# Two thirds of a depthwise convolution's taps as ScalarE products that VectorE adds, and a fifth seven-product pair in four early groups

## The chip, the cores and the metric

One Trainium2 chip, one core of it. The metric is the device time of one launch in microseconds, taken as the median of three runs. TensorE (PE), its weight loads (PEld), VectorE (DVE), ScalarE (ACT), GpSimd (POOL) and the DMA queue of SyncE (SP) each run their own instruction list in order and meet through semaphores.

## The reference, cut to what matters

```python
xn = rms_norm(h, norm_in_g)                       # 256 x 4096, float32
q, k, v, z_a, a_c, g_c, z_c = split(xn @ w_in)    # each 256 x 2048
y_a = rms_norm(chunked_attention(q, k, v), attn_out_g) * silu(z_a)

u = a_c * sigmoid(g_c)                            # convolution module
u = pad(u, 30 rows in front)
u = depthwise_conv(u, w_dw) + b_dw                # 31 taps a channel, causal
u = silu(layer_norm(u)) @ w_pw + b_pw
y_c = rms_norm(u, conv_out_g) * silu(z_c)

h = h + concat(y_a, y_c) @ w_out
h = h + sigmoid(rms_norm(h) @ w_ple_gate + b) * (p @ w_ple)
out = rms_norm(h, final_g)
```

256 rows, a width of 4096, 16 heads of 128. The change is in the taps of the depthwise convolution and in how four of the products `xn @ w_in` are computed.

## The kernel before

**Products.** Every big product is float32 by halves. A weight tile `wt` (128 rows, two column blocks of 512) is rounded by ScalarE to `wh` (`nc.scalar.copy`, L204), VectorE takes the rest `wl = wt - wh` (L205), and PE makes three matmuls of 128x512 for each block: high by high, low by high, high by low (L385). `wh` and `wl` have three buffers each, `wt` five.

**Groups.** `mixed_product` makes two column blocks at a time for both halves of the 256 rows. Its 4096 rows of weights go in 16 *pairs* of two 128-row blocks. A plain pair takes 2 x 4 x 3 = 24 matmuls. A pair with a mark in the order (`0+`, `4*`) is done in Winograd's way by seven products in place of eight: 7 x 3 = 21 matmuls, for which sums of weight blocks, `ua` and `ub`, are made first and split into `uh` and `ul`. With `*` VectorE makes the sums `ua` (L467, L468); with `+` a second DMA with accumulation, issued by GpSimd, does (L420, L421). The sums `ub` (L474, L475) are VectorE's in both. The other operand of such a pair is a combination of the blocks of xn, kept in `xS`; the combinations for pairs 8 and 10 come later than the others, from `more_combinations`.

**Stages.** The first part of the kernel is ten groups: `glu_conv(0)`, `glu_conv(1)`, q and k of heads 0 to 3, v of heads 0 to 7, then attention on heads 0 to 3, `glu_conv(2)`, and so on to the ninth, `heads((o_q, 3), (o_v, 2), order=early_five)`, and the tenth, which has the order `norm`. `glu_conv(1)` and the `heads` groups have the order `early` (four marked pairs, all `+`), `glu_conv(2)` and `(3)` `early_six` (six), the ninth `early_five` (five). Pointwise product, gated output, `w_out` and `w_ple_gate` follow, which the change does not touch.

**The convolution.** Each `glu_conv(c)` ends with the gated input transposed into `uT` (128 channels x 4 blocks x 256 rows) and puts 4 x 31 calls of `conv_tap` into the queue `later`: one VectorE instruction per block and tap, `cv += uT * dw` with the tap's weight as a per-channel scalar (L724; the first tap, with the bias, is L720). `fill(n)` takes the next n calls; `mixed_product` calls it after every pair, with the counts of `early_fills` or `six_fills`.

**What sets the order.** The program order is a wish: a scheduler at build time places each engine's instructions by when it takes them to be ready, so taps may move ahead of where `fill` puts them. `queued_behind(made)` keeps what is made in it behind given instructions; `recent` holds the last `wh` cast and the last `wl`. On each engine the order is fixed once built.

**Memory.** `home` is the tag `hd` with five buffers of 128 x 4 x 256, for `uT`, `kT`, `v`, the bias of the attention and sums. `stage` has two buffers, for the `z` of a group. `act` has eight buffers, for `cv`, `qT` and the late combinations `comb_x`.

Of the kernel before, what the change touches and what calls it, by code (L numbers as in the profile page):

```python
# [10 lines left out]
F32 = mybir.dt.float32  # L11
F32R = mybir.dt.float32r
AF = mybir.ActivationFunctionType
ALU = mybir.AluOpType
AX = mybir.AxisListType

P = 128
# [8 lines left out]
def hybrid_block(  # L26
# [23 lines left out]
    nc = tc.nc  # L50
    _, T, D = x.shape
# [5 lines left out]
    TAPS = w_dw.shape[1]  # L57
    PAD = TAPS - 1
# [23 lines left out]
    spool = pool("spool", 2, first_scratch, 1)  # L82
# [11 lines left out]
    o_q, o_k, o_v, o_za = 0, AW, 2 * AW, 3 * AW  # L94
# [85 lines left out]
    later = deque()  # L180

    def fill(n):
        for _ in range(min(n, len(later))):
            later.popleft()()
# [27 lines left out]
    recent = []  # L212

    @contextmanager
    def queued_behind(made):

        with ExitStack() as queued:
            for ins in made:
                queued.enter_context(tc.issue_after(ins.ins))
            yield  # L220
# [111 lines left out]
    early_five = units("1 3 5 0+ 7 9 2+ 11 4* 13 6+ 15 8* 10 12 14")  # L332
    early_six = units("1 3 5 0+ 7 2* 9 4+ 11 6* 13 8+ 15 10* 12 14")

    early_fills = (5, 6, 1, 5, 6, 1, 5, 6, 1, 5, 6, 1, 2, 5, 5, 4)
    six_fills = (6, 6, 1, 5, 1, 5, 1, 5, 1, 5, 1, 5, 1, 6, 7, 7)
    norm = units("1 3 5 7 9 11 0+ 13 2* 15 4+ 8 6* 10 12 14")
    norm_fills = (7, 8, 8, 8, 6, 4, 2, 3, 2, 3, 2, 2, 0, 6, 5, 5)
# [167 lines left out]
    tt, stt = nc.vector.tensor_tensor, nc.vector.scalar_tensor_tensor  # L506
# [174 lines left out]
    taps = w_dw[0].rearrange("t (b j q) -> (t b) j q", j=DWC, q=P)  # L681
# [10 lines left out]
    dw = spool.tile([P, KCW, TAPS], F32, name="dw", bufs=1)  # L692
# [25 lines left out]
    def conv_tap(cv, uT, i, b, k):  # L718
# [4 lines left out]
        else:  # L723
# [2 lines left out]
                cv[:, i, PAD - k :], ALU.mult, ALU.add,  # L726
            )

    def more_combinations(pair):

        if pair in (7, 9):
            c = (pair + 1) // 2
            xS[2 * c] = act.tile([P, 2, 2, T], F32R, tag="act", name="comb_x"), 0
            later.extendleft(reversed(combinations(c)))

    def glu_conv(c):
        if c == 0:
            sg, gate = scaled_pair(
                w_in0, o_a, o_g - o_a, first, r_x, (1,), begin=first_pairs
            )  # L740
        else:
            sg, gate = scaled_pair(
                w_in0, o_a + c * NB, o_g - o_a,
                *((early, r_x, early_fills) if c == 1 else (early_six, r_x, six_fills)),
                ahead=more_combinations if c == 2 else None,
            )
        for h in range(NH):
            nc.scalar.activation(gate[:, h, :], gate[:, h, :], AF.Sigmoid)
            tt(sg[:, h, :], sg[:, h, :], gate[:, h, :], ALU.mult)
        uT = spool.tile([P, 4, T], F32, tag="hd", name="uT", bufs=5)  # L750
        for pair in range(2):
            pt = tmp_psum()
            for i in range(2):
                for h in range(NH):
                    b = 2 * pair + i
                    nc.tensor.transpose(
                        pt[:, i * T + h * P : i * T + (h + 1) * P],
                        sg[:, h, b * P : (b + 1) * P],
                        ident,
                    )  # L760
            nc.scalar.copy(
                uT[:, 2 * pair : 2 * pair + 2, :], pt.rearrange("q (i t) -> q i t", t=T)
            )
        cv = act.tile([P, 4, T], F32, tag="act", name="cv")
        for i in range(4):
            for k in reversed(range(TAPS)):
                later.append(partial(conv_tap, cv, uT, i, 4 * c + i, k))
        conv.append(cv)


# [174 lines left out]
    home = dict(tag="hd", bufs=5)  # L945
# [9 lines left out]
    def heads(*parts, order=None, fills=early_fills, **kw):  # L955

        cols = [o + g * NB for o, g in parts]
        tiles = scaled_pair(
            w_in0, cols[0], cols[1] - cols[0], order or early, r_x, fills,
            homes=[home if o == o_v else dict(tag="stage") for o, _ in parts], **kw  # L960
        )
        for (o, g), t in zip(parts, tiles):
            if o == o_v:
                vs[g] = t
            else:
                (queries_of if o == o_q else keys_of)(g, t)
# [6 lines left out]

    n_g = H // GH
    assert n_g == CW // NB == 4
    glu_conv(0)
    glu_conv(1)
    load_bias(0)
    heads((o_q, 0), (o_k, 0))
    heads((o_v, 0), (o_v, 1))  # L980
    attention(0)
    glu_conv(2)
    load_bias(1)
    heads((o_q, 1), (o_k, 1))
    attention(1)
    glu_conv(3)
    load_bias(2)
    heads((o_q, 2), (o_k, 2))
    heads((o_q, 3), (o_v, 2), order=early_five)
    attention(2)  # L990
    layer_norm_swish()
# [24 lines left out]
    spool = upool = pool("lpool", 2, side=1)  # L1016
# [109 lines left out]
    for c0 in range(0, D // NB, 2):  # L1126
        for j in range(2):
            hc = act.tile([P, NH, NB], F32, tag="act", name="hc")
            c = c0 + j
# [5 lines left out]
        def on_helpers(helper):  # L1135
# [10 lines left out]
            ahead=y_ahead if c0 == 0 else before_last(h_ahead) if c0 + 2 == D // NB else None,  # L1146
            fills=(2,),
# [114 lines left out]
    def weigh(h, j):  # L1262
        pin(tt(z[h][j], hs[c0 + j][:, h, :], fgs[j], ALU.mult))
# [41 lines left out]
    halves = [slice(i * NB // 2, (i + 1) * NB // 2) for i in range(2)]  # L1305
# [46 lines left out]
```

## Time and profile before

| | |
|---|---|
| median of three runs | 2029.14 us (2028.86 to 2029.4) |
| the profiled execution | 2028.23 us |
| its span, first to last instruction | 2026.5 us |
| the second to ninth group with two attentions, 97.2 to 793.7 us of the span | 696.5 us |
| DMA, mean of the span | 215 GB/s |
| granted TensorE clock, mean | 0.998 |

All durations below come from the profiled execution. A row of a group view gives the operation, how many there are, their busy time together, the mean of one in ns, and the engine's idle time before them with what ended it. A row of the time line gives start, length, engine, line and operation, the number of instructions merged, and in brackets idle time before. Two instructions of one engine can overlap at their ends, so a merged row can be shorter than its number times the mean.

### The profile page before, as it was taken

How to read it: one execution, taken by the hardware profiler on the slowest of the kernel's cores; microseconds unless marked ns; L12 is line 12 of the kernel's file. 1: busy time of each engine (PE TensorE's matmuls, PEld its weight loads, DVE VectorE, ACT ScalarE, POOL GpSimd, SP SyncE). 2: the span in 40 equal slices, each digit the busy share in tenths (PEclk: the TensorE clock that was granted, in tenths of full speed). 3: DMA queues.
4: the chain of work that ended last, by engine and by line, in shares of the span. 5: the costliest groups of instructions: out<-in, count | busy, mean ns of one | idle time of the engine just before them, and what ended most of it. 6: DMA issues, size and time to landing. Idle time of an engine off the chain costs nothing.

```text
span 2026.5 us, 26195 instructions
## 1 busy us (share of the span) xinstructions
PE 2010.8 (99%) x9073; PEld 1654.4 (82%) x9073; DVE 1903.4 (94%) x2708; ACT 1215.0 (60%) x1583; POOL 46.9 (2%) x50
## 2 busy tenths in 40 slices
PE   9999999999999999999999999999999999999997
PEld 7888888888888888788888888888888888888876
DVE  7999999889999997888899999999999999999998
ACT  7655545655655555776556556666665666655555
POOL 0000000000000000000000000000000000000000
PEclk9999999999999999999999999999999999999999
DMA  8787878678678867456666666676666656666765
GB/s 295 222 238 234 255 217 250 177 247 240 188 221 246 252 198 241 156 177 209 196 208 207 208 204 211 208 239 210 203 211 197 208 194 201 208 218 207 231 207 180
DMA packets 171168, 436.70 MB, mean 215 GB/s; under 512 B 13966, under 2 KB 17182, under 8 KB 171034
## 3 DMA queue, kind: packets, MB, share of 16 engines
q1 hardware_dynamic: 161952, 417.93, 63.9%
q0 software_dynamic: 8432, 16.25, 4.8%
q8 instruction: 71, 1.16, 0.2%
q10 hardware_dynamic: 650, 0.84, 0.1%
q14 instruction: 63, 0.52, 0.1%
HBM read 430.77 MB, written 4.19 MB: 215 GB/s over the span
## 4 chain that ended last, share of the span: by engine, by line
PE 95%; DVE 3%; issue 1%; ACT 1%; DMA 0%; POOLq 0%; POOL 0%; ACTq 0%; SPq 0%; DVEq 0%
PE acc L385 73%; PE acc_P L385 17%; PE tmp_ps L170 1%; DVE cv L724 1%; PE acc L229 1%; DVE wl L205 1%; PE tmp_ps L893 0%; PE tmp_ps L877 0%; PE tmp_ps L911 0%; PE tmp_ps L916 0%; PE acc L373 0%; ACT wh L204 0%; PE tmp_ps L892 0%; DVE ul L205 0%; DMA xin<-in_x_dram 0%
## 5 line engine op out<-in xcount | busy, mean ns | idle before, releaser
L385 PE MATMUL acc<-wh,big_t 128*128 128x512 f32 x4154 | 1283.3, 391 | 0.6 <-DVE y_c L1043 0.4
L204 ACT CAST wh<-wt 128x1024 fp32r<-128x1024 f32 (+1 forms) x737 | 710.1, 974 | 523.3 <-PE acc L385 364.3
L385 PEld LDWEIGHTS acc<-wh,big_t 128*128 128x128 f32 x4154 | 777.0, 188 | 160.8 <-DVE y_c L1043 0.9
L205 DVE TENSOR_TENSOR wl<-wt,wh 128x1024 fp32r<-128x1024 f32 (+1 forms) x737 | 817.4, 1122 | 39.9 <-ACT wh L204 33.6
L385 PE MATMUL acc<-wl,big_t 128*128 128x512 f32 x2077 | 801.9, 391 | 0.1
L385 PEld LDWEIGHTS acc<-wl,big_t 128*128 128x128 f32 x2077 | 389.5, 188 | 82.5 <-DVE wl L205 1.8
L204 ACT CAST uh<-ua 128x1024 fp32r<-128x1024 f32 x174 | 182.9, 1052 | 91.1 <-DVE ua L468 46.3
L205 DVE TENSOR_TENSOR ul<-ua,uh 128x1024 fp32r<-128x1024 f32 x174 | 212.0, 1219 | 9.6 <-ACT uh L204 8.1
L724 DVE SCALAR_TENSOR_TENSOR cv<-uT,dw,cv 128x250 f32<-128x250 f32 (+19 forms) x480 | 203.6, 464 | 1.1
L385 PE MATMUL acc_P<-uh,big_t 128*128 128x512 f32 x528 | 161.8, 392 | 0.0
L204 ACT CAST uh<-ub 128x1024 fp32r<-128x1024 f32 x92 | 96.8, 1052 | 95.5 <-DVE ub L475 79.2
L205 DVE TENSOR_TENSOR ul<-ub,uh 128x1024 fp32r<-128x1024 f32 x92 | 112.2, 1220 | 6.7 <-ACT uh L204 5.6
L385 PEld LDWEIGHTS acc_P<-uh,big_t 128*128 128x128 f32 x528 | 98.0, 188 | 23.2 <-ACT uh L204 3.7
L385 PE MATMUL acc_P<-ul,big_t 128*128 128x512 f32 x264 | 101.3, 392 | 0.0
L467 DVE TENSOR_TENSOR ua<-wt 128x512 f32<-128x512 f32 x102 | 69.9, 685 | 17.3 <-DMA wt<-in_w_in_dram 10.7
L385 PE MATMUL acc<-uh,big_t 128*128 128x512 f32 x266 | 82.5, 390 | 0.0
L385 PE MATMUL acc_P<-wh,big_t 128*128 128x512 f32 x266 | 82.1, 389 | 0.0
L468 DVE TENSOR_TENSOR ua<-wt 128x512 f32<-128x512 f32 x102 | 69.6, 683 | 4.3 <-DMA wt<-in_w_in_dram 3.6
L385 PE MATMUL acc_P<-uh,comb_t 128*128 128x512 f32 x228 | 70.1, 390 | 0.1
L475 DVE TENSOR_TENSOR ub<-ub,wt 128x512 f32<-128x512 f32 x92 | 63.0, 685 | 0.8
L474 DVE TENSOR_TENSOR ub<-ua,wt 128x512 f32<-128x512 f32 x92 | 62.9, 683 | 0.3
L385 PEld LDWEIGHTS acc_P<-ul,big_t 128*128 128x128 f32 x264 | 49.3, 188 | 12.5 <-DVE ul L205 2.0
(243 smaller groups left out, 1485.5 us busy)
## 6 DMA issues: line engine op xcount, KB each, us to landing
wt<-in_w_in_dram SPq DMA_DIRECT2D x416, 512.0 KB, 4.5
wt<-in_w_out_dram SPq DMA_DIRECT2D x128, 512.0 KB, 4.3
wt<-in_w_ple_gate_dram SPq DMA_DIRECT2D x128, 512.0 KB, 4.2
wt<-in_w_pw_dram SPq DMA_DIRECT2D x32, 512.0 KB, 4.8
ua<-in_w_in_dram SPq DMA_DIRECT2D x31, 512.0 KB, 4.3
ua<-in_w_in_dram POOLq DMA_DIRECT2D x31, 512.0 KB, 8.7
wt<-in_w_in_dram SPq DMA_DIRECT2D x31, 256.0 KB, 2.8
hc<-in_x_dram SPq DMA_DIRECT2D x8, 512.0 KB, 4.7
```

The source lines that it names most:

```text
L170: nc.tensor.transpose(pt[:, i * T + h * P : i * T + (h + 1) * P], src[:, h, b] if len(src.shape) == 4 else src[:, h, b * P : (b + 1) * P], ...
L204: nc.scalar.copy(wh[:, :kc, :], wt[:, :kc, :]),
L205: nc.vector.tensor_tensor(wl[:, :kc, :], wt[:, :kc, :], wh[:, :kc, :].bitcast(F32), ALU.subtract),
L229: nc.tensor.matmul(acc, a, b[:, k, :], start=kb == 0 and kind == 0, stop=kb == kblocks - 1 and kind == 2,)
L385: nc.tensor.matmul(banks[name], a, b, start=name not in begun, stop=final and ends[name] == n and kind == 2 and not (left and name in "P2 ...
L467: plus(ua[:, 0], w0[:, 0], w0[:, 1])
L468: plus(ua[:, 1], w0[:, 1], w1[:, 1])
L474: plus(ub[:, 0], ua[:, 0], w1[:, 1])
L475: plus(ub[:, 1], ub[:, 0], w1[:, 0])
L724: nc.vector.scalar_tensor_tensor(cv[:, i, PAD - k :], uT[:, i, : T + k - PAD], dw[:, b, k : k + 1], cv[:, i, PAD - k :], ALU.mult, ALU.add,)
```

## The change

The taps go by threes. Of taps k, k+1 and k+2 the first is done as before by VectorE, one instruction per block. The products of the other two are made by ScalarE (`weigh`: `activation` with Identity and the tap's weight as `scale`), one per block, into one of two tiles `wu` of 128 x 4 x 256, and VectorE adds each tile to `cv` in one instruction over all four blocks (`add_weighed`). The add is queued one product later than its product. `weighted_in` says where the two tiles lie from then on, after it has drained what is pending. Four of the `heads` groups take the order `early_five` in place of `early`, with fill counts of their own, and `more_combinations` is called in `glu_conv(1)` in place of `glu_conv(2)`.

```diff
+    five_fills = (5, 7, 6, 2, 6, 5, 2, 5, 2, 5, 2, 5, 1, 2, 2, 2)
...
+    weighted, pending, halves = [], [], []
+    def weighted_in(*homes):
+        while halves:
+            fill(1)
+        while pending:
+            add_weighed(*pending[0][1:])
+        weighted[:] = homes
+    def weigh(cv, uT, b, k, blocks):
+        n = T + k - PAD
+        if blocks[0] == 0:
+            if not hasattr(weighted[0], "rearrange"):
+                weighted[:] = [spool.tile([P, 4, T], F32, name="wu", **kw) for kw in weighted]
+            weighted.append(weighted.pop(0))
+            pending.append((weighted[0], cv, k))
+            halves.append(k)
+        else:
+            halves.clear()
+        with queued_behind(recent[:1]):
+            for i in blocks:
+                nc.scalar.activation(
+                    pending[-1][0][:, i, :n], uT[:, i, :n], AF.Identity, scale=dw[:, b + i, k : k + 1]
+                )
+    def add_weighed(cv, k):
+        if pending and pending[0][1] is cv and pending[0][2] == k:
+            n = T + k - PAD
+            tt(cv[:, :, PAD - k :], cv[:, :, PAD - k :], pending.pop(0)[0][:, :, :n], ALU.add)
...
-                ahead=more_combinations if c == 2 else None,
+                ahead=more_combinations if c == 1 else None,
...
-        for i in range(4):
-            for k in reversed(range(TAPS)):
-                later.append(partial(conv_tap, cv, uT, i, 4 * c + i, k))
+        def taps(k, blocks):
+            later.extend(partial(conv_tap, cv, uT, i, 4 * c + i, k) for i in blocks)
+        taps(PAD, range(4))
+        adds = []
+        for k in range(0, PAD, 3):
+            for n in range(2):
+                for blocks in ((0, 1), (2, 3)):
+                    later.append(partial(weigh, cv, uT, 4 * c, k + 1 + n, blocks))
+                    taps(k, (2 * n + blocks[0] // 2,))
+                later.extend(adds)
+                adds = [partial(add_weighed, cv, k + 1 + n)]
+        later.extend(adds)
...
+    stage, five = dict(tag="stage"), dict(order=early_five, fills=five_fills)
     glu_conv(0)
+    weighted_in(home, home)
     glu_conv(1)
     load_bias(0)
-    heads((o_q, 0), (o_k, 0))
-    heads((o_v, 0), (o_v, 1))
+    weighted_in(home, home)
+    heads((o_q, 0), (o_k, 0), **five)
+    weighted_in(stage, stage)
+    heads((o_v, 0), (o_v, 1), **five)
     attention(0)
+    weighted_in(home, home)
     glu_conv(2)
     load_bias(1)
-    heads((o_q, 1), (o_k, 1))
+    weighted_in(home, home)
+    heads((o_q, 1), (o_k, 1), **five)
     attention(1)
+    weighted_in(home, home)
     glu_conv(3)
     load_bias(2)
-    heads((o_q, 2), (o_k, 2))
+    weighted_in(home, home)
+    heads((o_q, 2), (o_k, 2), **five)
+    weighted_in(stage, home)
     heads((o_q, 3), (o_v, 2), order=early_five)
```

How the change stands in the engines' lists is seen at three places. The first is ScalarE at the end of the first attention, which runs beside the first pairs of `glu_conv(2)`. `s` are the scores of a head (two exponentials each), `pT` the transposed probabilities, `qT` takes the head's output, `junk` the sum of squares, `wh` and `uh` are casts of weights. Before:

```order
L204 CAST wh<-wt 128x512
L920 ACTIVATE qT<-tmp_ps,den 128x128 x2
L904 ACTIVATE s,den<-s,nm 128x128
L904 ACTIVATE s,den<-s,nm 128x256
L204 CAST uh<-ua 128x1024
L913 COPY pT<-tmp_ps 128x384
L204 CAST wh<-wt 128x1024
L920 ACTIVATE qT<-tmp_ps,den 128x128 x2
L547 ACTIVATE junk,ssq_a<-qT 128x512 x2
L204 CAST wh<-wt 128x1024 x2
```

The same place with the change, from the second exponential of the last head on (line numbers are those of the changed kernel). Ahead of these rows stand the cast of 128x512, the pair of `qT`, four products in one row, `wu<-uT,dw 128x249 x4`, and the first exponential:

```order
L948 ACTIVATE s,den<-s,nm 128x256
L753 ACTIVATE wu<-uT,dw 128x251 x2
L957 COPY pT<-tmp_ps 128x384
L753 ACTIVATE wu<-uT,dw 128x251 x2
L753 ACTIVATE wu<-uT,dw 128x252
L964 ACTIVATE qT<-tmp_ps,den 128x128 x2
L548 ACTIVATE junk,ssq_a<-qT 128x512
L753 ACTIVATE wu<-uT,dw 128x252
L548 ACTIVATE junk,ssq_a<-qT 128x512
L204 CAST wh<-wt 128x1024
L204 CAST uh<-ua 128x1024
L753 ACTIVATE wu<-uT,dw 128x252 x2
```

Between the cast of 128x512 and the next cast `wh` of 128x1024 there are now ten products, and the pair of `qT` and the two sums of squares have come ahead of that cast, while `uh` has gone behind it. The next pair's casts have four products ahead of them.

The second place is VectorE in the group of q and k of heads 0 to 3, at its second marked pair, before:

```order
L205 TENSOR_TENSOR wl<-wt,wh 128x512
L474 TENSOR_TENSOR ua<-ua,wt 128x512
L724 SCALAR_TENSOR_TENSOR cv<-uT,dw,cv 128x242
L475 TENSOR_TENSOR ua<-ua,wt 128x512
L724 SCALAR_TENSOR_TENSOR cv<-uT,dw,cv 128x241
L720 TENSOR_SCALAR cv<-uT,dw,prm 128x256
L724 SCALAR_TENSOR_TENSOR cv<-uT,dw,cv 128x240
L205 TENSOR_TENSOR wl<-wt,wh 128x1024
```

The third is the same engine and group with the change, at its fourth and fifth marked pairs, `6+` and `8*`:

```order
L761 TENSOR_TENSOR cv<-cv,wu 128x4x255
L205 TENSOR_TENSOR ul<-ua,uh 128x1024
L205 TENSOR_TENSOR wl<-wt,wh 128x1024
L475 TENSOR_TENSOR ua<-ua,wt 128x512
L468 TENSOR_TENSOR ua<-wt 128x512
L476 TENSOR_TENSOR ua<-ua,wt 128x512
```

Where single taps stood between the splits there are now adds over four blocks, each of which needs four products of ScalarE, and splits `ul` and `wl` stand behind such an add.

Over the whole lists the change has 12 matmuls of 128x512 fewer (8988 against 9000). VectorE has 320 single taps fewer, 80 adds `cv<-cv,wu` of 128 x 4 x 227 to 255, 24 sums `ua` of 128x512, 8 splits `ul` of 128x1024 and 4 splits `wl` of 128x512 more, and 4 splits `wl` of 128x1024 fewer. ScalarE has 320 products `wu`, 8 casts `uh` and 4 casts `wh` of 128x512 more and 4 casts `wh` of 128x1024 fewer. Four loads and four accumulating loads `ua` are gone.

## The prediction

> **What bounds the kernel now.** I read the page's engine shares first, then the busy time by stage, then the chain of work that ended last, then single stretches of the time line.
>
> ```profile
> PE 2010.8 (99%) x9073; PEld 1654.4 (82%) x9073; DVE 1903.4 (94%) x2708; ACT 1215.0 (60%) x1583; POOL 46.9 (2%) x50
> ...
> 97.20:793.70 696.50, 696.26 (x3146) 575.33 (x3145) 667.18 (x1046) 383.46 (x469) 37.77 (x34) 1.00 0.78 231
> ...
> 183.00:268.50 85.50, 85.50 (x383) 70.80 (x382) 85.50 (x142) 44.25 (x50) 5.18 (x5) 1.00 0.83 240
> ...
> 693.27 17.00 PE acc L385 x75
> ...
> 1056.94 17.00 PE acc L385 x75
> ```
>
> The columns of the second and third row are the stretch, its length, and the busy time of PE, PEld, DVE, ACT, POOL, then clock, DMA share and GB/s. TensorE is busy throughout, but its ends are modelled, so the chain decides: 75 matmuls of 128x512 took 17.00 us at 693 us and again at 1057 us. That is 0.2267 us each, in a stage with convolution and in one without. TensorE sets the time, and only fewer matmuls or fewer gaps between them shorten it. VectorE is full in the group of q and k (85.50 of 85.50) yet TensorE does not wait for it: the scheduler pulls taps forward into any room. ScalarE has 313 us free in the eight groups.
>
> **The change part by part.** *TensorE.* Four groups get one more pair by 21 matmuls in place of 24: 12 fewer, 12 x 0.2267 = 2.72 us off the path. Nothing hides this gain.
>
> *VectorE.* The rows for what goes and what comes:
>
> ```profile
> L724 DVE SCALAR_TENSOR_TENSOR cv<-uT,dw,cv 128x250 f32<-128x250 f32 (+19 forms) x480 | 203.6, 464 | 1.1
> ...
> L810 DVE TENSOR_TENSOR sq<-sq 128x1024 f32<-128x1024 f32 x3 | 3.6, 1212 | 0.0
> ...
> L205 DVE TENSOR_TENSOR ul<-ua,uh 128x1024 fp32r<-128x1024 f32 x174 | 212.0, 1219 | 9.6 <-ACT uh L204 8.1 <-PE acc L385 1.2
> ...
> L205 DVE TENSOR_TENSOR wl<-wt,wh 128x512 fp32r<-128x512 f32 x133 | 90.8, 683 | 0.4 <-ACT wh L204 0.3
> ...
> L467 DVE TENSOR_TENSOR ua<-wt 128x512 f32<-128x512 f32 x102 | 69.9, 685 | 17.3 <-DMA wt<-in_w_in_dram 10.7 <-DMA wt<-in_w_out_dram 4.9 <-DMA wt<-in_w_ple_gate_dram 1.4
> ```
>
> 320 taps go at 203.6/480 = 0.424 us: 135.7 us. The 80 adds have 4 x 241 = 964 elements in the mean; between 0.685 us at 512 and 1.212 us at 1024 elements that is 1.15 us, 92 us in all. The fifth pair, and `*` in place of one `+`, cost 24 sums at 0.685, 8 splits at 1.219 and 4 at 0.683, less 4 at 1.219: 16.4 + 9.8 + 2.7 - 4.9 = 24 us. Net 20 us less, 647 of 694 us. It is worth nothing by itself, as TensorE did not wait for it.
>
> *ScalarE.* No row shows a product of 128x241 from SBUF with a column as scale. The nearest are:
>
> ```profile
> L846 ACT CAST big_t<-cv 128x256 fp32r<-128x256 f32 x16 | 5.4, 401 | 0.2 <-PE acc L385 0.2
> ...
> L836 ACT ACTIVATE cv<-cv,prm 128x256 f32<-128x256 f32 x16 | 8.6, 592 | 0.0
> ...
> L204 ACT CAST wh<-wt 128x512 fp32r<-128x512 f32 x133 | 82.6, 621 | 83.0 <-PE acc L385 47.9 <-issue 20.3 <-ACT wh L204 7.8
> ...
> L534 ACT ACTIVATE z<-z,r_x 128x512 f32<-128x512 f32 x30 | 20.6, 718 | 23.3 <-DVE z L514 21.9 <-DVE z L516 1.4
> ...
> L920 ACT ACTIVATE qT<-tmp_ps,den 128x128 f32<-128x128 f32 x32 | 10.0, 362 | 5.6 <-PE tmp_ps L918 5.5
> ```
>
> Below, a plain cast of 256 elements at 0.40 us; above, 0.59 us with two column operands. Identity with one column operand costs 0.718 at 512 against 0.621 for a cast, 0.10 more, so 0.49 at 241 elements. In a row two overlap: the pair of `qT` below takes 0.63 us where one takes 0.362, so 0.27 from start to start and 0.09 saved. I take 0.40 a product: 128 us, bounds 0.31 and 0.59 (99 and 189 us). With 7 us of casts for the fifth pairs ScalarE comes to 518 of 694 us, 75%. On the mean it has room.
>
> The Trainium skill, "ScalarE: Activation LUTs", Rules for kernel authors, puts multiplications on VectorE and not on ScalarE. The rows agree that a product here costs about what the VectorE tap cost; by that rule alone the change would not pay, and rival 4, at 2032.5 us, is its mechanism.
>
> *Where the products stand in the way.* A cast that is late holds VectorE's split, and that TensorE. At most places a burst of four products (1.6 us) meets a margin of several us. The exception is the end of an attention, where ScalarE is busy already. Before:
>
> ```profile
> 372.81 0.62 ACT L920 ACTIVATE qT<-tmp_ps,den 128x128 f32<-128x128 f32 x2 [0.42 <-PE tmp_ps L918]
> 374.47 0.40 ACT L904 ACTIVATE s<-s,nm 128x128 f32<-128x128 f32 x1 [1.04 <-DVE nm L903]
> ...
> 376.35 0.47 ACT L913 COPY pT<-tmp_ps 128x384 f32<-128x384 f32 x1
> 376.72 1.05 ACT L204 CAST wh<-wt 128x1024 fp32r<-128x1024 f32 x1
> 377.94 0.63 ACT L920 ACTIVATE qT<-tmp_ps,den 128x128 f32<-128x128 f32 x2 [0.18 <-PE tmp_ps L918]
> 378.46 0.63 ACT L547 ACTIVATE junk<-qT 128x512 bf16<-128x512 f32 x1
> ...
> 379.85 1.99 ACT L204 CAST wh<-wt 128x1024 fp32r<-128x1024 f32 x2
> ...
> 375.34 0.27 PE L911 MATMUL tmp_ps<-ident,s 128*128 128x128 f32 x1
> ...
> 381.88 0.62 PE L385 MATMUL acc<-wh,big_t 128*128 128x512 f32 x2
> 382.33 0.39 PE L385 MATMUL acc<-wl,big_t 128*128 128x512 f32 x1
> ```
>
> TensorE took the cast of 376.72 at 381.88, 4.1 us after it was done. Now four products start at 373.43 where ScalarE was idle for 1.04 us: the exponential starts at 375.1 in place of 374.47, and the transpose that stood at 375.34 loses about 0.4 us. Then exponentials to 376.1, two products to 376.9, `pT` to 377.4, three products to 378.6, the pair of `qT` to 379.2, two squares and a product (0.75 + 0.4 + 0.75) to 381.1, the cast to 382.1. TensorE, 0.4 late, wants it at 382.3: just in time. But the split takes 1.2 us more, to 383.4, and is wanted at 382.33 + 0.4: 0.65 late. With 0.2 for an add ahead of the next split I take 1.3 us. The second attention has one product ahead of the last exponentials and about nine behind; by the same steps 0.4 + 0.2 = 0.6 us. The third has none. Sum 1.9 us.
>
> Bounds: none at all, or products at 0.59. That adds 0.19 x 14 at the first attention (ten, and four ahead of the next casts) and 0.19 x 8 at the second, 4.2 us, all of it late. Some products in the first attention also wait until the attention has done with its keys and bias, whose buffers they take; behind them stand the last head's exponentials and casts, and this is within the 1.3 us.
>
> *Moved at no cost.* The combinations for pairs 8 and 10 come a group earlier, in `glu_conv(1)`, into buffers of `act` that the inputs have left; cover is VectorE's queue of taps, and without it they cost the same work as later. Four accumulating loads fewer on POOL's queue, and four on SP's, take load off queues that run ahead. The bias loads on SP wait for a buffer of `hd`; behind them stand weight loads, covered by five `wt` buffers.
>
> *Sum.* -2.72 + 1.9 = -0.8 us. The profiled execution has 2028.23 us with 1.7 us around its span and would come to 2027.4; it lies 0.9 us below the median of 2029.14, so the median comes to 2028.3 us.
>
> **The rivals.** *1, forecast: most of the gain is given back in two attentions*, 2028.3 (2026.8 to 2030.5). *2, all products are hidden*: 2029.14 - 2.72 = 2026.4. For it: VectorE is full in the groups before, and TensorE keeps its pace. Against: the steps above. *3, the attentions even get better.*
>
> ```profile
> 373.08 0.82 PE L385 MATMUL acc<-wh,big_t 128*128 128x512 f32 x2
> ...
> 373.96 0.63 PE L385 MATMUL acc<-wh,big_t 128*128 128x512 f32 x2
> ```
>
> After each head's scores two matmuls take 0.82 in place of 0.63 us. Were 0.2 us at eight heads to go as well, 2026.4 - 1.6 = 2024.8. Against: nothing in the change touches the scores, and ScalarE gets fuller there.
>
> *4, ScalarE is the local bound*: products at 0.59 with no overlap give 2028.3 + 4.2 = 2032.5, and more if the eight products behind each new `uT` delay casts too.
>
> *5, slower: VectorE stops at its adds.* An add waits for four products on an engine that works in order and may itself be behind a cast that waits for TensorE; behind the add stand the splits.
>
> ```profile
> 183.03 2.72 DVE L538 SCALAR_TENSOR_TENSOR z<-acc,r_x,z 128x512 f32<-128x512 f32 x4
> ...
> 186.80 1.29 DVE L749 TENSOR_TENSOR z<-z 128x512 f32<-128x512 f32 x2
> 188.01 2.35 DVE L205 TENSOR_TENSOR wl<-wt,wh 128x1024 fp32r<-128x1024 f32 x2
> 190.28 2.00 DVE L724 SCALAR_TENSOR_TENSOR cv<-uT,dw,cv 128x240 f32<-128x240 f32 x5
> ```
>
> Start to start a split of 1024 costs 1.13, a sum of 512 elements 0.60, a scaled sum 0.66, a tap 0.39 us. The group of q and k then needs 37 x 1.13 + 25 x 0.60 + 4 x 0.66 + 27 x 0.39 + 11 adds x 1.07 = 81.7 us of the 85.50 - 0.68 = 84.8 it has: 3.1 us to spare. Eleven adds use that up at 0.28 us of waiting each. At 0.5 us a group loses 2.4 us, four groups 9.6: 2029.14 - 2.72 + 9.6 = 2036.0. For it: VectorE has no idle time in these groups. Against: the add stands one product later, and ScalarE is at 75%.
>
> **How the numbers follow.** Chances: forecast 0.56, rival 2 0.17, rival 3 0.05, rival 4 0.06, rival 5 0.16. A measurement of this kernel tells about 0.2%, 4.06 us, from no change. Faster than 2025.08 is rival 3 and the edge of rival 2, 0.06. Slower than 2033.20 is rival 5 and half of rival 4, 0.20. The rest, 0.74, is the same. The range 2025.8 to 2033.0 leaves out rival 3 and most of rival 5.
>
> **What would show it.** TensorE's matmuls at 0.2267 us outside the attentions and 12 fewer; 320 products near 0.49 us, 0.40 start to start; VectorE's busy time in the eight groups near 647 and ScalarE's near 518 us; idle time before `cv` adds with ScalarE as releaser under 0.28 us each; gaps on TensorE at the last head of attentions 0 and 1 on splits of a cast that stands behind products. Wrong would be a gap at every marked pair (rival 5), or products near 0.59 us (rival 4).

## The result and the profile after

| kernel | median us | range, runs | ratio, 95% interval |
|---|---|---|---|
| before | 2028.83 | 2027.70 to 2030.59, 17 | |
| changed | 2032.82 | 2031.81 to 2034.22, 17 | 1.0020 [1.0013, 1.0026] |

The changed kernel is 4.0 us slower, where 0.8 us faster was forecast. The profiled execution took 2032.45 us with a span of 2030.4 us (before 2028.23 and 2026.5).

First the page of the changed kernel: the engines' shares, and the groups of the products, the adds, and the taps that stay.

```profile
PE 2014.3 (99%) x9061; PEld 1651.0 (81%) x9061; DVE 1893.6 (93%) x2500; ACT 1339.7 (66%) x1911; POOL 42.3 (2%) x46
...
L753 ACT ACTIVATE wu<-uT,dw 128x246 f32<-128x246 f32 (+19 forms) x320 | 133.8, 489 | 2.1 <-DVE cv L761 2.0
...
L761 DVE TENSOR_TENSOR cv<-cv,wu 128x908 f32<-128x908 f32 (+9 forms) x80 | 92.6, 1157 | 7.9 <-ACT wu L753 6.3
...
L725 DVE SCALAR_TENSOR_TENSOR cv<-uT,dw,cv 128x226 f32<-128x226 f32 (+9 forms) x160 | 69.3, 461 | 0.4
```

There are 12 matmuls fewer (9061 for 9073), the products take 0.489 us and the adds 1.157 us, and VectorE is idle only 7.9 us before the 80 adds, 0.10 us each. The unit prices are those of the forecast. Now the stretches, with their length, the busy time of PE, PEld, DVE, ACT, POOL, then clock, DMA share and GB/s: the second to ninth group together, then the four groups that got a fifth pair.

```profile
97.70:796.70 699.00, 698.64 (x3134) 570.62 (x3133) 656.99 (x837) 507.13 (x797) 33.00 (x30) 1.00 0.74 225
183.10:268.70 85.60, 85.40 (x378) 69.51 (x377) 82.50 (x105) 62.00 (x95) 4.07 (x4) 1.00 0.73 227
268.70:355.00 86.30, 86.30 (x387) 70.91 (x386) 80.50 (x97) 63.46 (x100) 3.66 (x3) 1.00 0.73 223
446.30:531.90 85.60, 85.59 (x379) 69.84 (x378) 84.77 (x109) 64.70 (x101) 3.96 (x4) 1.00 0.77 233
625.00:710.80 85.80, 85.74 (x379) 69.87 (x378) 84.91 (x109) 64.80 (x101) 5.17 (x5) 1.00 0.77 234
```

VectorE and ScalarE come to 657 and 507 us of 699 (forecast 647 and 518 of 694). The last three of the four groups before (the row of the first, 183.00:268.50, stands in the prediction):

```profile
268.50:354.80 86.30, 86.30 (x391) 71.59 (x390) 85.95 (x143) 45.22 (x51) 4.87 (x4) 1.00 0.79 231
444.80:530.60 85.80, 85.75 (x382) 70.72 (x382) 85.73 (x141) 45.81 (x51) 5.17 (x5) 1.00 0.83 242
622.70:708.40 85.70, 85.68 (x382) 70.65 (x381) 85.65 (x140) 45.75 (x51) 5.18 (x5) 1.00 0.82 241
```

No group is 3 x 0.2267 = 0.68 us shorter: the four take 85.6, 86.3, 85.6 and 85.8 us where they took 85.5, 86.3, 85.8 and 85.7. TensorE reads as busy all the time, since ends of matmuls are modelled; the time is lost between the starts. The table sums, for every group, what the step from one start of a 128x512 matmul to the next has beyond 0.2267 us, with the small matmuls of transposes and attention at their full time. (The traces hold 8521 and 8509 matmuls of this size, 12 apart as they should be, so no step is long because a record is missing. Each group is taken from VectorE's first scaled sum of the group ahead to its own.)

```
us beyond 0.2267 a matmul       before   changed   difference
first group (glu_conv(0))        10.49     11.01      +0.52
glu_conv(1)                       1.43      0.95      -0.48
q, k of heads 0 to 3              0.92      2.10      +1.18
v of heads 0 to 7                 1.83      2.47      +0.64
attention(0) itself               7.38      7.50      +0.12
glu_conv(2) behind it             0.18      0.98      +0.80
q, k of heads 4 to 7              1.26      1.83      +0.57
attention(1) itself               9.30      9.42      +0.12
glu_conv(3) behind it             0.00      0.88      +0.88
q, k of heads 8 to 11             1.26      1.99      +0.73
ninth group                       1.77      2.42      +0.65
norm group and all behind        44.71     45.26      +0.55
sum                              80.52     86.81      +6.29
```

12 x 0.2267 = 2.72 us are saved, and 6.29 us are lost: 3.12 in the four five-pair groups, 1.68 at the marked pairs of `glu_conv(2)` and `(3)`, 0.65 in the ninth group, only 0.24 in the attentions. The first and the last row, +1.07 together, differ by as much between the kernels below, although their VectorE and ScalarE instructions are the same (10.2 to 11.3 us for the first group alone), so they are not counted against the change.

One such gap, from the time line of the changed kernel in the first q and k group: TensorE, ScalarE and VectorE at the first marked pair (`uh` is the cast of the sum of weights, `ul` its split).

```profile
205.43 0.61 PE L386 MATMUL acc_P<-uh,comb_t 128*128 128x512 f32 x2
205.88 0.61 PE L386 MATMUL acc<-uh,big_t 128*128 128x512 f32 x2
206.69 0.51 PE L386 MATMUL acc_P<-ul,comb_t 128*128 128x512 f32 x1 [0.20 <-DVE ul L205]
207.03 0.40 PE L386 MATMUL acc<-ul,big_t 128*128 128x512 f32 x1
...
202.04 1.05 ACT L204 CAST wh<-wt 128x1024 fp32r<-128x1024 f32 x1 [1.39 <-PE acc L386]
203.00 1.04 ACT L204 CAST uh<-ua 128x1024 fp32r<-128x1024 f32 x1
...
203.18 1.18 DVE L761 TENSOR_TENSOR cv<-cv,wu 128x992 f32<-128x992 f32 x1
204.28 1.22 DVE L205 TENSOR_TENSOR wl<-wt,wh 128x1024 fp32r<-128x1024 f32 x1
205.42 1.22 DVE L205 TENSOR_TENSOR ul<-ua,uh 128x1024 fp32r<-128x1024 f32 x1
```

The same place before:

```profile
205.37 0.61 PE L385 MATMUL acc_P<-uh,comb_t 128*128 128x512 f32 x2
205.82 0.39 PE L385 MATMUL acc_P<-ul,comb_t 128*128 128x512 f32 x1
...
200.18 1.05 ACT L204 CAST uh<-ua 128x1024 fp32r<-128x1024 f32 x1
...
201.64 1.22 DVE L205 TENSOR_TENSOR ul<-ua,uh 128x1024 fp32r<-128x1024 f32 x1
```

Before, the cast of the sum ran at 200.18 and its split was done at 202.86, 3 us ahead of TensorE. In the changed kernel the cast stands behind a `wh` cast that waits 1.39 us for TensorE to free a buffer, and the split stands behind an add of 1.18 us and a split for the next pair: it is done at 206.64, and TensorE takes it at 206.69. VectorE waits for nothing here; it works without a break, in an order that no longer gives TensorE what it needs next. This first marked pair is the same in both kernels. What differs ahead of it, besides the adds and products, is the fill count: `early_fills` puts one call of the queue ahead of each marked pair, `five_fills` six ahead of the first and five ahead of each of the others.

### The profile page after: what moved, and what is told of

Read it like the earlier page. It is cut to its first block, busy times and chain, and to the rows that moved or that the text cites. A ratio compares the mean times of both kernels' runs of the same rounds, so it can differ in the third digit from the quotient of the medians.

```text
span 2030.4 us, 26256 instructions
## 1 busy us (share of the span) xinstructions
PE 2014.3 (99%) x9061; PEld 1651.0 (81%) x9061; DVE 1893.6 (93%) x2500; ACT 1339.7 (66%) x1911; POOL 42.3 (2%) x46
## 4 chain that ended last, share of the span: by engine, by line
PE 94%; DVE 3%; issue 1%; ACT 1%; DMA 1%; POOLq 0%; ACTq 0%; POOL 0%; DVEq 0%
PE acc L386 72%; PE acc_P L386 18%; PE tmp_ps L170 1%; DVE wl L205 1%; PE acc L229 1%; DVE ul L205 0%; PE tmp_ps L937 0%; ACT wh L204 0%; PE tmp_ps L921 0%; PE tmp_ps L955 0%; DMA wt<-in_w_ple_gate_dram 0%; DVE cv L846 0%; PE tmp_ps L960 0%; PE acc L374 0%; PE tmp_ps L125 0%
## 5 line engine op out<-in xcount | busy, mean ns | idle before, releaser
L386 PE MATMUL acc<-wh,big_t 128*128 128x512 f32 x4098 | 1267.5, 391 | 0.2
L386 PEld LDWEIGHTS acc<-wh,big_t 128*128 128x128 f32 x4098 | 766.8, 188 | 159.1 <-ACT big_t L156 0.6
L386 PE MATMUL acc<-wl,big_t 128*128 128x512 f32 x2049 | 790.8, 392 | 0.1
L386 PEld LDWEIGHTS acc<-wl,big_t 128*128 128x128 f32 x2049 | 384.3, 188 | 81.3 <-DVE wl L205 1.6
L204 ACT CAST uh<-ua 128x1024 fp32r<-128x1024 f32 x182 | 191.1, 1051 | 72.2 <-DVE ua L469 58.1
L205 DVE TENSOR_TENSOR ul<-ua,uh 128x1024 fp32r<-128x1024 f32 x182 | 221.6, 1218 | 7.8 <-ACT uh L204 7.2
L753 ACT ACTIVATE wu<-uT,dw 128x246 f32<-128x246 f32 (+19 forms) x320 | 133.8, 489 | 2.1 <-DVE cv L761 2.0
L761 DVE TENSOR_TENSOR cv<-cv,wu 128x908 f32<-128x908 f32 (+9 forms) x80 | 92.6, 1157 | 7.9 <-ACT wu L753 6.3
L468 DVE TENSOR_TENSOR ua<-wt 128x512 f32<-128x512 f32 x110 | 75.4, 685 | 13.6 <-DMA wt<-in_w_in_dram 6.9
L469 DVE TENSOR_TENSOR ua<-wt 128x512 f32<-128x512 f32 x110 | 75.2, 684 | 1.9 <-DMA wt<-in_w_in_dram 1.9
L725 DVE SCALAR_TENSOR_TENSOR cv<-uT,dw,cv 128x226 f32<-128x226 f32 (+9 forms) x160 | 69.3, 461 | 0.4
```

The lines of the kernel that those rows point to most:

```text
L204: nc.scalar.copy(wh[:, :kc, :], wt[:, :kc, :]),
L205: nc.vector.tensor_tensor(wl[:, :kc, :], wt[:, :kc, :], wh[:, :kc, :].bitcast(F32), ALU.subtract),
L386: nc.tensor.matmul(banks[name], a, b, start=name not in begun, stop=final and ends[name] == n and kind == 2 and not (left and name in "P2 ...
L468: plus(ua[:, 0], w0[:, 0], w0[:, 1])
L469: plus(ua[:, 1], w0[:, 1], w1[:, 1])
L725: nc.vector.scalar_tensor_tensor(cv[:, i, PAD - k :], uT[:, i, : T + k - PAD], dw[:, b, k : k + 1], cv[:, i, PAD - k :], ALU.mult, ALU.add,)
```

## The experiments

All were compared with the kernel before in the same set of runs, 10 or 11 runs each against 21 to 33 of before. "Gaps of the four" is the table's sum over q and k of heads 0 to 3, 4 to 7, 8 to 11 and v of heads 0 to 7: 5.28 us before, 8.39 changed. The gaps of a kernel come from one profiled execution. Where two kernels have the same VectorE and ScalarE instructions in one of the four groups, in the same order, the gaps repeat within about 0.2 us, with one exception: in the first q and k group they were once 2.10 and once 3.01 us. A late load can add 1 to 3 us to a group, as seen below.

### The two halves of the change, each alone

Taps alone: the changed kernel without `**five`, and the late combinations in `glu_conv(2)` again.

```diff
-    heads((o_q, 0), (o_k, 0), **five)
+    heads((o_q, 0), (o_k, 0))
```

> Products and adds as in the change, but the four groups keep four marked pairs (12 matmuls more than the changed kernel) and the late combinations come in glu_conv(2) as before. The changed kernel stands 4.0 us above the one before (2032.8 against 2028.8). Theory A (the prediction's: products cost 1.9 us in two attentions, nothing elsewhere): 2028.8 + 1.9 = 2030.7 us. Theory B (the splits of the sums ub come late at marked pairs, behind adds, taps or products; about 0.8 us a group in the changed kernel, with 5 marked pairs in four groups): the gaps are still there at the 4 marked pairs that are left, 2028.8 + 1.9 + 0.8 x 4 to 5 groups x 4/5 + 0.8 x 2 = 2034 to 2035 us. Theory C (the fifth pair's own sums and splits on a full VectorE give the gain back): 2030.7 us as by A, and the excess in the q and k groups falls back to 0.2 to 0.55 us.

Measured: 2029.46 us against 2029.41, ratio 1.0000 [0.9991, 1.0009]. Gaps of the four 4.85 us; `glu_conv(2)` and `(3)` behind their attentions 0.25 and 0.52 us. All 320 products and 80 adds together cost nothing that can be measured, less than theory A and much less than theory B had it.

Fifth pair alone: the kernel before, with `order=early_five` in the four groups and the late combinations in `glu_conv(1)`. The fill counts stay those of `early_fills`.

```diff
-    heads((o_q, 0), (o_k, 0))
+    heads((o_q, 0), (o_k, 0), order=early_five)
```

> The kernel before with all taps on VectorE, but the fifth marked pair in the four groups and the late combinations a group earlier. 12 matmuls fewer. Theory A: 2028.8 - 2.7 = 2026.1 us. Theory B (products and adds make the splits late): 2026.1 us as well, perhaps 0.3 more for a fifth place per group. Theory C (the fifth pair's sums on a full VectorE): the 24 us more on VectorE meet 667 of 694 us busy, so that gaps come back as large as in the changed kernel or larger: 2029.5 us or more.

Measured: 2033.01 against 2029.41, ratio 1.0018 [1.0009, 1.0027]. Twelve matmuls fewer make the kernel 3.6 us slower, with no product in it. Gaps of the four 8.22 us, as in the changed kernel: 2.94 us more than before, where 2.72 us of matmuls are saved. Another 1.1 us lies in the two groups with attentions, and about 2.6 us from the norm group on, where the kernels are the same and the gaps differ by up to 4 us between the profiles; so how much of the 3.6 us is the fifth pair's is not known. The four groups:

```profile
183.60:268.20 84.60, 84.42 (x375) 69.37 (x375) 80.37 (x120) 45.61 (x51) 3.95 (x4) 1.00 0.79 234
268.20:354.20 86.00, 85.98 (x386) 70.78 (x385) 85.90 (x137) 45.62 (x52) 3.66 (x3) 1.00 0.73 216
445.40:531.30 85.90, 85.88 (x380) 69.83 (x379) 85.44 (x135) 46.84 (x52) 3.96 (x4) 1.00 0.77 235
624.40:710.20 85.80, 85.52 (x378) 69.47 (x377) 85.41 (x135) 46.86 (x52) 3.96 (x4) 1.00 0.76 232
```

In the last three VectorE is at 85.90 of 86.00, 85.44 of 85.90 and 85.41 of 85.80 us. In the first it has 4.2 us of idle time, and the gaps still rise from 0.92 to 1.59 us, so the sum of free time in a group does not decide alone. By its time theory C held: the half that was to bring the gain is the half that loses. But `early_fills` is made for four marked pairs: it puts six calls ahead of `4*` and five ahead of `6+`, where every marked pair had one before. In the first two groups the longest gap behind the transposes lies at `4*` (0.34 and 0.18 us). How much of the loss is the counts' doing this run does not tell.

### Which engine has no room

Adds without products: the adds read `uT` in place of `wu`, and `weigh` makes no product.

> The changed kernel without the 320 ScalarE products; the adds of 128x4x241 stay and read uT itself, so VectorE has the changed kernel's work and never waits for ScalarE there. What is left out: the products of two thirds of the taps. Theory A (ScalarE's products in the attentions are the only loss): 2028.8 - 2.7 = 2026.1 us. Theory B1 (VectorE: splits stand behind long adds of 1.16 us and taps): only the 1.9 us of the attentions go, 2032.8 - 1.9 = 2030.9 us, and the gaps at marked pairs remain. Theory B2 (ScalarE: casts of sums stand behind products): all of it goes, 2026 to 2027 us. Theory C: 2030.9 us like B1.

Products without adds: each add covers one column.

```diff
-            tt(cv[:, :, PAD - k :], cv[:, :, PAD - k :], pending.pop(0)[0][:, :, :n], ALU.add)
+            one = slice(PAD - k, PAD - k + 1)
+            tt(cv[:, :, one], cv[:, :, one], pending.pop(0)[0][:, :, :1], ALU.add)
```

> The changed kernel with its 320 products on ScalarE, but each add takes one column of the four blocks only (4 elements a partition), so VectorE loses about 80 x 1.0 = 80 us and still waits for the same products. What is left out: the adds' other columns. Theory A: 2026.1 + 1.9 = 2028.0 us. Theory B1 (long adds ahead of splits): gaps at marked pairs go, the attentions stay: 2028 us, perhaps less. Theory B2 (casts behind products): gaps stay, 2032 to 2033 us. Theory C (a full VectorE): 2028 us, as VectorE is 80 us emptier.

Measured: adds only 2028.34, ratio 0.9998 [0.9989, 1.0006], gaps of the four 6.69 us; products only 2028.65, ratio 0.9996 [0.9987, 1.0005], gaps of the four 6.18, of which 1.42 are one late weight load in the third. Either relief takes 4.5 to 4.9 us from the changed kernel, by the ratios, so neither B1 nor B2 is right alone: a marked pair's sums go from VectorE to ScalarE and back, and work on either side can delay them. VectorE's side weighs more: with adds only, 1.4 us of the 3.1 us of added gaps stay; with products only, nothing but the late load does. The groups with products only, in the same order as above:

```profile
183.20:267.70 84.50, 84.50 (x378) 70.04 (x377) 72.78 (x103) 62.03 (x96) 3.95 (x4) 1.00 0.78 234
267.70:353.20 85.50, 85.50 (x386) 70.95 (x386) 72.44 (x100) 63.52 (x100) 3.66 (x3) 1.00 0.75 224
444.70:530.90 86.20, 85.05 (x379) 69.92 (x378) 75.90 (x110) 64.34 (x101) 3.96 (x4) 1.00 0.76 232
623.40:708.00 84.60, 84.60 (x379) 70.10 (x378) 76.10 (x111) 64.53 (x101) 3.96 (x4) 1.00 0.78 237
```

With 8 to 13 us of idle VectorE in a group and all products in place, three of the four are 0.8 to 1.1 us shorter than before. In these groups this is the forecast's gain, seen; in the time of the whole kernel it is not clear of the interval. The profiled execution was the longest of its eleven (2031.15 us), and its late load need not be in the others.

Fifth pair alone with every third tap left out (160 of 480):

> The fifth pair alone, all taps on VectorE, as in the second experiment (2033.0 us), but every third tap (160 of 480, 62 us of VectorE from start to start) is left out. Theory V: with room on VectorE the pairs are worth their 12 matmuls: 2029.4 - 2.7 = 2026.7 us, gaps of the four groups near 5.3 us or below. Theory F (a fifth pair loses its gain whatever VectorE has to do, through its loads or its place in the order): 2032 to 2033 us.

Measured: 2029.05 against 2029.59, ratio 0.9998 [0.9989, 1.0007], gaps of the four 6.40 us. It is 4 us better than the fifth pair alone, against theory F, but not at the 2026.7 us of theory V. The scheduler pulls the taps that are left forward, so VectorE stays full in the three q and k groups; the room turned up in v and in the groups behind. The first two of the four groups:

```profile
183.00:268.50 85.50, 85.50 (x382) 70.84 (x382) 84.97 (x133) 45.90 (x52) 3.95 (x4) 1.00 0.78 231
268.50:353.60 85.10, 84.77 (x382) 70.05 (x382) 72.35 (x95) 45.81 (x51) 3.66 (x3) 1.00 0.75 225
```

In v, with 12.7 us of idle VectorE, the steps at and between the marked pairs lose next to nothing (0.12 us, as before); the other 2.32 of its 2.44 us of gaps stand at the transposes at its start, where it was 1.71 before. In q and k of heads 4 to 7 and 8 to 11 (VectorE at 85.2 of 85.7 us) a gap of 0.33 us remains at `4*`. The first q and k group loses nothing either (0.92 us, as before), although VectorE is just as full there: a full VectorE goes with the loss in most groups, not in all.

### Where the taps and the pairs stand

Four forms of the changed kernel with the same matmuls: fewer fills at the last marked pairs, all five pairs with `+`, the pairs further apart, and every tap and add kept behind the last VectorE split.

```diff
-    five_fills = (5, 7, 6, 2, 6, 5, 2, 5, 2, 5, 2, 5, 1, 2, 2, 2)
+    five_fills = (5, 7, 6, 1, 6, 5, 1, 4, 1, 3, 1, 3, 0, 2, 2, 2)
```

> The changed kernel with smaller fill counts in the four groups at and between the last three marked pairs (1 4 1 3 1 3 0 in place of 2 5 2 5 2 5 1); the taps that are left go to the groups after, which have room on VectorE. Same work in all. Before 2029 us, changed 2032.8 us. Theory V (at a marked pair VectorE has, start to start, four splits of 0.6, 1.13, 1.13, 1.13 and four sums of 0.60, 6.4 us, against 21 matmuls or 4.76 us on TensorE; tap work placed there makes the last split late): part of the 3.1 us of added gaps in the four groups goes, 2030 to 2031.5 us. Theory S (ScalarE's casts stand behind products, VectorE's taps do not matter): products per marked pair fall in the same proportion, so the same; this run alone does not tell V from S. Theory F (it is the number of marked pairs alone, whatever stands between): 2032.8 us.

```diff
+    five_plus = units("1 3 5 0+ 7 9 2+ 11 4+ 13 6+ 15 8+ 10 12 14")
```

> The changed kernel, but the pairs 4 and 8 of the four groups have the sums ua made by an accumulating DMA (+) and not by VectorE (*), as the other three have. VectorE loses 8 x 2 sums at 0.60 us, 9.6 us in all, 1.2 us at each of these pairs; ScalarE keeps its work. Theory V: the chain of such a pair falls from 6.4 to 5.2 us and most of the gaps at pairs 4 and 8 go (about 0.5 of the 0.8 us added in each group): 2030.5 us. Theory S: nothing of it goes, 2032.8 us. A third way: the accumulating loads come late, and it is 2034 us or more.

```diff
+    five_apart = units("1 3 0+ 5 7 2+ 9 11 4* 13 15 6+ 10 8* 12 14")
```

> The changed kernel with the five marked pairs of the four groups set further apart: two plain pairs between each of the first four, from the third pair on, and one before the last; the fill counts are moved along with them (59 in all as before). Theory V: a plain pair gives VectorE 5.44 - 2.26 = 3.2 us, two give 6.4 us, enough for the chain of 6.4 us and for the taps: gaps fall by 2 to 3 us, 2030 us. Theory F: 2032.8 us.

```diff
     def conv_tap(cv, uT, i, b, k):
+        with queued_behind(recent[1:]):
```

> The changed kernel, but every tap and add is kept behind the last VectorE split written before it, in all groups, so that none can be pulled forward into the sums and splits of the pair ahead of it in the program. Same instructions. Theory V: the last split of a marked pair no longer stands behind tap work of later fills; gaps in the four groups fall, 2030 to 2031 us. Theory S: they stay, 2032.8 us. Against V, too: taps that cannot be pulled forward into idle time come later and may push on the next pair, 2033 us or more.

Measured against 2029.57 us, with the gaps of the four groups in the order q k, v, q k, q k:

```
                 median us   ratio, 95% interval         gaps of the four
changed, above     2032.82   1.0020 [1.0013, 1.0026]     2.10 2.47 1.83 1.99
fewer fills        2031.72   1.0010 [1.0001, 1.0019]     2.39 2.09 1.49 1.99
all +              2032.07   1.0014 [1.0005, 1.0023]     2.83 1.94 1.38 1.50
further apart      2033.81   1.0021 [1.0012, 1.0030]     2.78 4.01 1.27 1.29
taps kept behind   2034.29   1.0024 [1.0015, 1.0033]     2.31 2.75 2.03 2.27
```

None of the four ratios is clear of the changed kernel's interval, so only the gaps tell the forms apart. In the last two groups, setting the pairs apart takes the gaps back to those of before (1.26), and leaving the sums to the DMA most of the way, as theory V has it; fewer fills take back 0.34 us in one of the two and nothing in the other. The order set apart stands, with taps by threes, in three more kernels below, and its gaps in these two groups are 1.26 to 1.32 us in all four. In the first two groups it makes the gaps larger. The time line of the kernel with the pairs apart (its profiled execution, 2035.89 us, was the longest of its eleven), VectorE at the last marked pair of v (`ua` are the sums), and behind it TensorE's row in its view of waits (total, times, longest):

```profile
329.55 0.69 DVE L469 TENSOR_TENSOR ua<-wt 128x512 f32<-128x512 f32 x1 [0.56 <-DMA wt<-in_w_in_dram]
...
333.68 0.69 DVE L470 TENSOR_TENSOR ua<-wt 128x512 f32<-128x512 f32 x1 [1.09 <-DMA wt<-in_w_in_dram]
```

```profile
PE acc_P L387 <- DVE ul L205: 1.6, 1, 1.6
```

A `*` pair needs its weight tiles at its start, and here VectorE waited 0.56 and 1.09 us for tiles to land; TensorE then waited 1.6 us. The tiles come into five buffers that VectorE's own splits and sums release, so a late VectorE can also make late loads. Keeping the taps behind the splits helped nowhere (the gaps of the four come to 9.36 us); that a tap which may not fill an idle moment comes later and costs more would fit, but is not shown.

### The attentions

The changed kernel with the last taps of the second and third block on VectorE; 56 products and 14 adds become 56 taps (the expectation below counts 76 and 19).

```diff
-        for k in range(0, PAD, 3):
+        n_by_threes = {1: 21, 2: 18}.get(c, PAD)
+        for k in range(0, n_by_threes, 3):
...
+        for k in range(n_by_threes, PAD):
+            taps(k, range(4))
```

> The changed kernel, but the last taps of the second and the third convolution block (k from 21 and from 18 on) go by VectorE alone, so that ScalarE has no product from the first softmax to the last head in attentions 0 and 1. Theory A for the attention term (1.94 us of added gaps in the two attention groups come from products ahead of the exponentials, transposes and casts): both groups fall back towards 7.6 and 9.3 us of gaps, 2031 us. Rival: the gaps there come from the place of VectorE's work, and with 76 taps for 19 adds VectorE has 10 us more to do: 2033 us or more.

Measured: 2031.67 against 2029.59, ratio 1.0010 [1.0001, 1.0019]. The two groups with attentions fall from 18.78 to 16.66 us of gaps (before 16.84), as expected, and the gaps in `glu_conv(2)` and `(3)` are gone. The time falls by less, about 1.1 us, as the first q and k group has 3.01 us of gaps here, though its VectorE and ScalarE instructions are those of the changed kernel. So the 1.9 us went with these products and adds, but the place was not the softmax. They are not the only cause: the fifth pair alone, with no product at all, has 0.46 and 0.65 us in `glu_conv(2)` and `(3)`, where 0.18 and none stood before.

### Putting the parts together

Each of the four groups in its best form (first q and k group with four pairs, v with five `+`, the last two apart):

> The changed kernel with each group in the form that left the fewest gaps so far: q and k of heads 0 to 3 with four marked pairs as before, v with five pairs all of +, the other two q and k groups with five pairs set apart. 9 matmuls fewer than before, 2.04 us. Gaps of the four groups from the single runs 0.94 + 1.94 + 1.27 + 1.29 = 5.4 us, as before (5.28). If the groups stand for themselves, what is left is the attentions' 0.8 to 1.9 us: 2029.4 - 2.0 + 0.2 + 0.8 to 1.9 = 2028.4 to 2029.5 us, the same as before. If a gain in one group only moves the gaps into the next, 2031 us or more.

The same without products in the attentions:

> Both of the two kernels above in one. If the terms add: 2029.4 - 2.04 + 0.2 + 0 to 0.5 = 2027.5 to 2028 us, below both kernels. If not: as the mix alone or slower.

Measured: 2029.71 (ratio 1.0003 [0.9994, 1.0012]) and 2029.31 us (1.0000 [0.9992, 1.0009]) against 2029.59: the same as before. In the profile of the second, v alone has 2.6 us more of gaps than in the first; its view of waits has ScalarE's cast waiting 2.6 us for an accumulated sum (this profiled execution took 2031.02 us, 1.7 us over the median). Then the fifth pair in the last two groups only, set apart, first with split taps and none in the attentions, then with all taps on VectorE:

> The best parts so far: the fifth pair, set apart, only in the q and k groups of heads 4 to 7 and 8 to 11, no ScalarE products in the attentions, the other groups with four marked pairs. 6 matmuls fewer than before, 1.36 us. If the groups stand for themselves (gaps of these two groups 1.3 us each, as before; attentions 17.1 against 16.8 us): 2029.5 - 1.4 + 0.3 = 2028.4 us, or 0.05% below before, which a single comparison cannot tell from none. If it is 2030 us or more, each pair still moves its gain elsewhere.

> The same two groups with the fifth pair set apart, but all taps on VectorE as before, so VectorE has no room there. Theory V: their gaps stay at 2 us or more each (the second experiment's 2.0 and 2.3 us), the gain is given back: 2029.5 to 2031 us. If the place of the pairs alone does it and VectorE's load does not matter: gaps of 1.3 us each, group times of 85.0 us, 2028.2 us.

Measured against 2028.89 us: 2027.28 (ratio 0.9993 [0.9984, 1.0002]) and 2028.95 (0.9999 [0.9990, 1.0008]). The two groups, split taps first, then VectorE's:

```profile
443.80:528.80 85.00, 85.00 (x379) 69.79 (x378) 83.72 (x107) 64.28 (x101) 3.96 (x4) 1.00 0.74 228
621.20:706.30 85.10, 85.10 (x379) 69.92 (x379) 83.79 (x108) 64.38 (x101) 3.96 (x4) 1.00 0.76 229
```

```profile
445.90:531.30 85.40, 85.40 (x378) 69.66 (x378) 85.11 (x132) 45.62 (x51) 2.74 (x3) 1.00 0.72 226
623.90:709.40 85.50, 85.36 (x379) 69.85 (x379) 85.10 (x132) 46.93 (x53) 4.17 (x4) 1.00 0.76 235
```

With 1.3 us of idle VectorE each group keeps the whole gain of its pair (85.0 and 85.1 for 85.8 and 85.7 us, gaps 1.29 and 1.28); with 0.3 to 0.4 us two thirds of it go again (gaps 1.73 and 1.69 for 1.26 before, less than the 2 us that theory V named). Order and fill counts are the same in both, so the taps make the difference; whether by VectorE's time alone or also by where single taps and adds stand, the two do not tell. The first of the two has the lowest median of all, but its interval reaches 1: that it beats the kernel before is likely, not shown.

## Why the prediction was wrong

**The step that failed** is the first: "12 x 0.2267 = 2.72 us off the path. Nothing hides this gain." In the changed kernel the four groups lose 3.12 us of gaps against the 2.72 us saved, and the fifth pair alone, with no other change to the work, makes the kernel 3.6 us slower. That 2032.82 us lies inside the stated range, by 0.2 us, is luck: no part of the sum leads there, and the time moved the other way. Taking seven products for eight shortens TensorE's share of a marked pair to 21 x 0.2267 = 4.76 us and raises VectorE's: from the forecast's own durations, start to start, a `*` pair is one split of 0.60, three of 1.13 and four sums of 0.60, 6.4 us, and a `+` pair, without two of the sums, 5.2 us. VectorE falls behind TensorE at every marked pair and catches up at plain ones (2 x 1.13 us against 24 x 0.2267 = 5.44). Before, VectorE was as full, but the four pairs were all `+` and stood two plain pairs apart. With the fifth, two are `*`, and from the second on they stand one plain pair apart, which leaves less time to catch up. The rows that were shown did carry this: the VectorE budget of the q and k group, 81.7 of 84.8 us, stood under rival 5, but was read as a sum over the group. With VectorE busy for 80.5 to 84.9 us of 85.6 to 86.3, the groups lost 0.6 to 1.2 us each, and the one with the most to spare (v) no less than the full ones. That VectorE's work at the marked pairs is the step is shown by emptying it: with the adds' columns left out, the loss is gone from all four groups but for one late load.

**VectorE's 20 us.** "It is worth nothing by itself, as TensorE did not wait for it" was wrong in the same way. Before, TensorE did wait little; with a fifth pair set apart, the room that split taps leave on VectorE lets the pair pay in two groups (gaps 1.3 us with split taps, 1.7 without).

**The attentions.** The 1.9 us of the forecast and the 1.92 us measured agree by accident of place. The exponential came later, as traced: 375.38 us, where 375.1 was forecast and 374.47 stood before (the stretch starts 0.2 us later).

```profile
373.79 1.69 ACT L753 ACTIVATE wu<-uT,dw 128x249 f32<-128x249 f32 x4
375.38 0.39 ACT L948 ACTIVATE s<-s,nm 128x128 f32<-128x128 f32 x1
```

But the attentions lost 0.12 us each, not 1.3 and 0.6. The loss lay behind them, at the marked pairs of `glu_conv(2)` and `(3)`. It went when products and adds of the same convolution blocks became taps, but part of it is there without any product too (fifth pair alone, 1.1 us). "At most places a burst of four products (1.6 us) meets a margin of several us" holds as long as the four groups have four marked pairs (taps alone: same time) and fails with five, in the group shown by a split that came 0.3 us late.

**Prices.** Product 0.489 us (forecast 0.49), adds 1.157 (1.15), 12 matmuls: right. In a row products start 0.40 us apart (four in the 1.69 us above: 1.69 less 0.49, by three). Rival 4 fell with that. By the Trainium skill, "ScalarE: Activation LUTs", Rules for kernel authors, the multiplications should have stayed on VectorE (the page gives a speed in bf16 as the reason, the data here are float32); taken alone, moving them made no difference here (1.0000 [0.9991, 1.0009]).

**Rival 5** came nearest: slower, in these groups, with VectorE's fullness as the reason. Its mechanism was not what happened. Its sign, gaps at marked pairs, was there, but adds waited 0.10 us each, under its 0.28, and the four groups lose as much without any add.

**Still open.** In the first two groups VectorE has 3.1 and 5.8 us of idle time in the changed kernel, and they still lose 1.18 and 0.64 us; with the pairs apart they lose more. The fill counts are a rival that no run tests: none gives five marked pairs the one call ahead of each that four had (fewer fills leaves 6, 5, 4, 3 and 3). In the last two groups they are not what decides, as the pairs set apart pay there with three to six calls ahead of each; in the first two, and in the fifth pair alone, they may be. Nor is it known how much of the rest is late loads and how much is VectorE. The weight buffers are released by VectorE (before, the load queue waited for a split `wl` 146 times in the eight groups, 273 us in all), so a late VectorE can make late loads; but with products only, where VectorE was busy for 75.9 of 86.2 us, a `*` pair still waited 2.17 us for its weights. A sixth weight buffer, which might part the two, was not tried.

## What to carry to other kernels

Count a saving on the bounding engine against the engine that prepares its operands pair by pair, not by the sum over the stage: where preparing takes longer (6.4 us) than using (4.76 us), an engine with 3 us free in 85 can come too late at every pair. Try each half of a combined change alone; here one half was free and the other lost, and the one that lost was the one with the safe-looking arithmetic. Here a lighter VectorE paid only where its new room lay next to the work that was late.

## What the runs showed of the hardware

A stall of TensorE costs more than the wait: the matmul that follows the delayed one starts late as well. In the gap above, 206.69 to 207.03 is 0.34 us where the pace is 0.2267; 0.11 us more stood behind most of the stalls in the runs, with waits from 0.03 to 1.8 us. By this estimate three waits of 0.1 us cost 0.63 us where one of 0.3 us costs 0.41, so that small waits at many pairs weigh more than their length.
